# Attention B's table for permuting maxima becomes a constant of the whole kernel, loaded first, and mixer A's half outputs share one buffer

## The chip, the cores and the metric

The kernel runs on one core of a Trainium2 chip. A core has a matrix engine (TensorE, PE in the rows below, with PEld for its weight loads), a vector engine (VectorE, DVE), a scalar engine (ScalarE, ACT), a general engine (GpSimd, POOL), a sequencer that mostly issues transfers (SyncE, SP), and 16 DMA engines that the queues of all of them share. The on-chip memory is laid out in 128 partitions; matrix products end in eight banks of PSUM. The metric is the device time of one execution in microseconds (us); less is better.

## The reference, cut to what matters

One layer of a decoder over 2048 tokens of width 1024, in float32. The width is split into two groups of eight heads of 64. Mixer A is causal sliding-window attention; mixer B is dilated attention of three branches, whose maxima and denominators must be exchanged between the branches' token orders. Then output projection, a SwiGLU feed-forward part (FFN, 2816 wide) and a last normalisation.

```python
def hybrid(x):
    z = rmsnorm(x, g_attn) @ w_in + b_in          # q, k, v of A and B
    a = sliding_window_sink_gqa(qA, kA, vA, sinks)
    b = dilated_mixture(qB, kB, vB, rel_table)     # branches (128,1), (512,4), (2048,16)
    h = x + concat(rmsnorm(a, g_out_a), rmsnorm(b, g_out_b)) @ w_o
    u = rmsnorm(h, g_ffn)
    return rmsnorm(h + (silu(u @ w_gate) * (u @ w_up)) @ w_down, g_final)
```

## The kernel before

The program is written for a tile framework. A scheduler of the framework, which keeps a model of times of its own, sets the order of the instructions on each engine once, when the kernel is built; within an engine they then run strictly in that order, each waiting for semaphores. A change of pools or of one load can therefore give other orders far away from the changed lines.

The stages, by the time in the profiled execution: the input projection (up to about 310 us, with parts of mixer A's preparation), mixer A with the rest of the projections (to about 570), attention B (to about 880), the output projection (to about 1100), the first half of the FFN in two groups of tokens, `t2=0` (about 1105 to 1555) and `t2=1` (to about 1975), and the second half of the FFN to the end.

`shared_constants` loads small tensors into the pool `c0`, which lives through the whole kernel. `attend_b` opens pools of its own; its pool `cb` holds `sel`, 128 x 156 float32 (78 KB, 624 B in each partition), whose four parts are the 0/1 matrices with which `joint_max` and the sums after it permute and spread maxima among partitions. In `joint_max`, DVE builds `ex` from the maxima `nm` and `sel` (L658, L670), PE multiplies it by a part of `sel` into `pp` (L661, L672), and DVE takes the maxima (L680 to L683). ACT's exponentials of attention B (L454) wait for them. The logits of both mixers are made by L432 (PE) and L436 (DVE, which adds the bias and takes the row maxima).

SBUF is full at that place: `cb` lies where one of mixer A's work buffers (`hl` of L479) lay, so the load of `sel` can only be issued when mixer A's last units are through. It stands in SP's queue behind the loads of the first heads' `v` (L631) and ahead of the next `q` (L610).

Mixer A goes through 32 units. At the end of each, ACT copies one half of the output bank to `rawa` (L562), DVE adds the other half to it into `sums` (L565), and POOL's queue stores `sums` (L566). `rawa` has the tag `half` of the pool `qa`, which has two buffers for each tag.

In the first half of the FFN (`quads`, L1073 to L1099) both products, by the gate weights (g) and the up weights (u), are made by a Strassen-like scheme of seven products for each block of columns j, eleven blocks for each group of tokens. For each j and each of g and u there are three PSUM banks X, Y and Z; a product is 12 matmuls of 128 x 512 (four slices, three terms of split precision). Y is read twice on the way, so PE may not go on with it before DVE has read it:

```python
            product(Y, S, w, "S2", True, False)
            nc.vector.tensor_add(u2, Y, c1)          # L1082
            product(Z, S, w, "S1", True, False)
            product(Y, S, w, "S3", False, False)     # waits for u2
            nc.vector.tensor_add(u3, Y, c1)          # L1086
            nc.vector.tensor_add(c22, Z, u3)         # L1088
            product(X, S, w, "A12", False, True)
            product(Y, S, w, "A22", False, True)     # waits for u3
            nc.vector.tensor_add(c21, Y, c1)         # L1094
            product(Z, S, w, "S4", False, True)
            nc.vector.tensor_add(c12, Z, u2)         # L1098
```

DVE and ACT also prepare the weights of the next j: two raw halves of 512 KB for each of g and u are loaded by SP (`wraw_g`, `wraw_u`, L1044) into a ring of buffers that they share with the halves of `draw` (fold_down, L1135 to L1141, a third weight folded once and stored as `wT`); DVE forms `T1` to `T4` (L1050, L1052, L1056, L1060); ACT rounds (`wh`, L1035) and DVE takes the rest (`wl`, L1037). POOL, with `t2=0`, multiplies the results (L1164 to L1177) and SP stores them (`actS`, L1157). `first_quads` does the first product of `t2=0` in another way, slice by slice (L1108).

Of the kernel before, what the change touches and what calls it, by code (L numbers as in the profile page):

```python
# [10 lines left out]
F32 = mybir.dt.float32  # L11
# [6 lines left out]
P = 128  # L18
S = 2048
D = 1024  # L20
HD = 64
# [102 lines left out]

def shared_constants(tc, cp, g_out_a, g_out_b):
    nc = tc.nc
    ident = cp.tile([P, P], F32, name="ident")
    make_identity(nc, ident)  # L130
    half = cp.tile([P, 8], F32, name="half")
    nc.vector.memset(half, -0.5)
    ones = cp.tile([P, 1], F32, name="ones1")
    nc.vector.memset(ones, 1.0)
    gout = cp.tile([P, KC], F32, name="gout")
    nc.gpsimd.dma_start(gout[:, 0:4], g_out_a[0].rearrange("(k p) -> p k", p=P))
    nc.gpsimd.dma_start(gout[:, 4:8], g_out_b[0].rearrange("(k p) -> p k", p=P))
    return ident, half, ones, gout


def mixers(tc, consts, x, g_attn, w_in, b_in, sinks, rel, rope, mask_a, onehot, sel, sc):
    ident, half = consts[:2]
    with ExitStack() as e1:
        project(tc, e1, ident, half, x, g_attn, w_in, b_in, sinks, rel, rope, mask_a, onehot, sc)
    attend_b(tc, ident, sel, sc)


def project(tc, es, ident, half, x, g_attn, w_in, b_in, sinks, rel, rope, mask_a, onehot, sc):
# [269 lines left out]
def logits(nc, pools, blocks, nm, init):  # L418

    wk, _, ps_s, _, _ = pools  # L420
    nb = len(blocks)
    small = all(b["own"] for b in blocks)
    per = nb if small else 2
    nk = P if small else 2 * P
    for b0 in range(0, nb, per):
        bl = blocks[b0:b0 + per]
        s = ps_s.tile([P, per, nk], F32, tag="s", name="s")
        t = wk.tile([P, per, nk], F32, tag="t", name="t")
        for i, b in enumerate(bl):
            n = P if b["own"] else 2 * P  # L430
            for m in range(2):
                nc.tensor.matmul(s[:, i, :n], b["q"], b["k"][m], start=(m == 0), stop=(m == 1))  # L432
        for i, b in enumerate(bl):
            n = P if b["own"] else 2 * P
            c = b["col"]
            nc.vector.tensor_tensor_reduce(  # L436
                out=b["kv"](t[:, i, :n]), in0=b["kv"](s[:, i, :n]), in1=b["tab"], scale=-0.125, scalar=init,
                op0=ALU.add, op1=ALU.min, accum_out=nm[:, c:c + 1])
            b["t"] = t[:, i, :n]
# [20 lines left out]
def transposed(nc, ident, pools, blocks, ps):  # L460

    _, hp, _, ps_t, _ = pools
    nb = len(blocks)
    hl = hp.tile([P, 2, 2 * nb, P], F32R, tag="hl", name="hl")
    small = all(b["own"] for b in blocks)
    per = nb if small else 2
    for b0, p in zip(range(0, nb, per), ps):
        pt = ps_t.tile([P, 4, P], F32, tag="pt", name="pt2")
        slots = []
        for i, b in enumerate(blocks[b0:b0 + per]):  # L470
            for hfn in range(1 if b["own"] else 2):
                sl = i if small else 2 * i + (1 if b["own"] else hfn)
                nc.tensor.transpose(pt[:, sl, :], p[:, i, hfn * P:(hfn + 1) * P], ident)  # L473
                slots.append(sl)
        a, z = slots[0], slots[-1] + 1
        off = b0 if small else 2 * b0
        hi, lo = hl[:, 0, off + a:off + z, :], hl[:, 1, off + a:off + z, :]
        nc.scalar.copy(hi, pt[:, a:z, :])  # L478
        nc.vector.tensor_sub(lo, pt[:, a:z, :], hi.bitcast(F32))  # L479
    return hl  # L480
# [19 lines left out]
class MixerA:  # L500
# [22 lines left out]
    def unit(self, jg, g, h):  # L523
        nc, sc = self.nc, self.sc
        j0 = max(4 * jg - 1, 0)
        nj = 4 * jg + 4 - j0
        if h == 4 * g:
            self.k = []
            for s2 in range(2):
                k = self.kp.tile([P, 5 * P], F32R, tag=f"k{s2}", name=f"ka{s2}")  # L530
                for d in range(2):
                    nc.sync.dma_start(k[d * 64:d * 64 + 64, :nj * P].bitcast(F32),
                                      sc.kA[g, s2, :, j0 * P:(j0 + nj) * P])
                self.k.append(k)
            self.v = self.kp.tile([P, 5, P], F32R, tag="v", name="va")
            nc.sync.dma_start(self.v[:, :nj].bitcast(F32),
                              sc.vA[j0 * P:(j0 + nj) * P, g].rearrange("(j p) e -> p j e", p=P))
        if h % 2 == 0:
            self.q = self.qp.tile([P, 2, 512], F32R, tag="q", name="qa")
            nc.sync.dma_start(self.q.bitcast(F32),  # L540
                              sc.qA[h:h + 2].rearrange("h s d n -> (s d) h n")[:, :, jg * 512:(jg + 1) * 512])
        qs = self.q[:, h % 2]
        raw = self.qp.tile([HD, 512], F32, tag="half", name="rawa")
        blocks = []
        for i in range(4):
            j = 4 * jg + i
            own = j == 0
            a = j - (0 if own else 1) - j0
            blocks.append(dict(
                q=qs[:, i * P:(i + 1) * P], own=own, col=j,  # L550
                k=[k.rearrange("p (j r a) -> p r j a", r=16, a=8)[:, :, a:j + 1 - j0, :] for k in self.k],
                tab=self.mska[:, :, 8:16] if own else self.mska, kv=k1v,
                tv=ident_f if own else t1v, pv=ident_f if own else p1v))
        nm, l = self.nm[:, h], self.l[:, h]
        logits(nc, self.pools, blocks, nm, self.nsnk[:, h:h + 1])
        o = self.ps_o.tile([P, 512], F32, tag="o", name="oa")
        hl = transposed(nc, self.ident, self.pools, blocks, exps(nc, self.pools, blocks, nm, l, 2))
        weighted(nc, blocks, hl, self.v, [4 * jg + i - j0 for i in range(4)], 0 if jg else None,
                 lambda oc, w, m: (o[:, oc * P:(oc + w) * P], m), True, True)


        nc.scalar.copy(raw, o[HD:])  # L562
        r4 = raw.rearrange("p (j t n) -> p t j n", j=4, t=4)
        sums = self.qp.tile([HD, 512], F32, tag="sums", name="sums")
        nc.vector.tensor_tensor(out=sums.rearrange("p (t j n) -> p t j n", t=4, j=4), in0=o[:HD].rearrange("p (j t n) -> p t j n", j=4, t=4), in1=r4, op=ALU.add)  # L565
        nc.gpsimd.dma_start(sc.oA[:, h * HD:(h + 1) * HD, jg * P:(jg + 1) * P].rearrange("t p n -> p t n"),  # L566
                            sums.rearrange("p (t n) -> p t n", t=4))
# [12 lines left out]
        nc.gpsimd.dma_start(self.sc.fA.rearrange("t h (j n) -> (h j) t n", j=16), ft)  # L580


def attend_b(tc, ident, sel_in, sc):

    nc = tc.nc
    with ExitStack() as es:
# [5 lines left out]
        rp = es.enter_context(tc.tile_pool(name="rp", bufs=2, reuse_waits="tile"))  # L592
        st = es.enter_context(tc.tile_pool(name="st", bufs=2, reuse_waits="tile"))
        cp = es.enter_context(tc.tile_pool(name="cb", bufs=1, reuse_waits="tile"))
        sel = cp.tile([P, 28 + P], F32, name="sel")
        nc.sync.dma_start(sel, sel_in)
        mod8, div8, div32, mod32 = sel[:, 0:8], sel[:, 8:24], sel[:, 24:28], sel[:, 28:]
        rcs = cp.tile([P, NH // 2, NT, 2, 4], F32, name="rcs")
        ps_s = es.enter_context(tc.tile_pool(name="ps_s", bufs=2, space=PSUM, reuse_waits="tile"))
# [196 lines left out]
def phase3(tc, consts, x, w_o, g_ffn, w_gate, w_up, w_down, g_final, out, sc):  # L796
    nc = tc.nc
    with ExitStack() as es:
        ps = es.enter_context(tc.tile_pool(name="ps3", bufs=8, space=PSUM, reuse_waits="tile"))
        with tc.tile_pool(name="rw3", bufs=4, reuse_waits="tile") as rw:  # L800
            project_out(tc, consts, ps, rw, x, w_o, g_ffn, sc)
            ffn_in(tc, ps, rw, w_gate, w_up, w_down, sc)
        ffn_out(tc, consts, ps, w_down, g_final, out, sc)
# [9 lines left out]
def project_out(tc, consts, ps, rw, x, w_o, g_ffn, sc):  # L813

    nc = tc.nc
    ident, half, ones, gout = consts
    xr = x[0].rearrange("(i r) d -> r i d", r=16)
    wov = w_o[0].rearrange("(k p) n -> p k n", p=P)
    with ExitStack() as es:
        pool = lambda name, bufs: es.enter_context(tc.tile_pool(name=name, bufs=bufs, reuse_waits="tile"))  # L820
        op, wp0, slot, wp1, cp, sp, xp, hp = (pool(n, b) for n, b in (
            ("op", 2), ("wo30", 1), ("slot", 6), ("wo31", 1), ("c3", 1), ("s3", 2), ("x3", 8), ("hst", 2)))
# [484 lines left out]
def hybrid_layer(tc, x, g_attn, w_in, b_in, sinks, rel_table, g_out_a, g_out_b, w_o, g_ffn, w_gate, w_up, w_down,  # L1307
                 g_final, rope, mask_a, onehot, sel, out):
    with tc.tile_pool(name="scr", bufs=1, space=DRAM) as pool, tc.tile_pool(name="c0", bufs=1) as cp:
        sc = make_scratch(pool)  # L1310
        consts = shared_constants(tc, cp, g_out_a, g_out_b)
        mixers(tc, consts, x, g_attn, w_in, b_in, sinks, rel_table, rope, mask_a, onehot, sel, sc)
        phase3(tc, consts, x, w_o, g_ffn, w_gate, w_up, w_down, g_final, out, sc)


# [20 lines left out]
```

## Time and profile before

| | |
|---|---|
| time, median of 3 runs | 2415.98 us (2415.11 to 2416.64) |
| the profiled execution: its own time | 2418.04 us |
| its span in the trace | 2416.3 us |
| mean granted clock of TensorE | 0.976 of full speed |
| PE busy | 2310.1 us, 96% of the span |
| DVE, ACT, POOL busy | 1619.8, 1062.1, 498.5 us |

The span is from the first to the last instruction of the profiled execution; the other 1.7 us lie around it. "Idle before" of an instruction is the time in which its engine did nothing ahead of it, with what ended that. The granted clock is 1.00 at 2.4 GHz and 0.50 at 1.2 GHz. Durations of neighbouring instructions overlap a little: a DVE instruction of 128 x 512 is shown with 0.68 us and the next begins 0.60 us after its start.

### The profile page before, as it was taken

How to read it: one execution, taken by the hardware profiler on the slowest of the kernel's cores; microseconds unless marked ns; L12 is line 12 of the kernel's file. 1: busy time of each engine (PE TensorE's matmuls, PEld its weight loads, DVE VectorE, ACT ScalarE, POOL GpSimd, SP SyncE). 2: the span in 40 equal slices, each digit the busy share in tenths (PEclk: the TensorE clock that was granted, in tenths of full speed). 3: DMA queues.
4: the chain of work that ended last, by engine and by line, in shares of the span. 5: the costliest groups of instructions: out<-in, count | busy, mean ns of one | idle time of the engine just before them, and what ended most of it. 6: DMA issues, size and time to landing. Idle time of an engine off the chain costs nothing.

```text
span 2416.3 us, 34033 instructions
## 1 busy us (share of the span) xinstructions
PE 2310.1 (96%) x11765; PEld 1961.3 (81%) x11765; DVE 1619.8 (67%) x3155; ACT 1062.1 (44%) x2371; POOL 498.5 (21%) x446
## 2 busy tenths in 40 slices
PE   7999999997999979997999999899999999999998
PEld 7987788886999968885778878678888878888887
DVE  5335555545999986658777777696676747557555
ACT  5323355552978883434322323342323334444442
POOL 2311200001333220103223232323232330000000
PEclk9999999996999989999999999999999999999999
DMA  7657565559788667734544444343233339668663
GB/s 218 209 180 220 156 182 150 147 138 227 174 194 202 139 202 218 251 143 174 175 161 149 161 148 156 124 139 103 93 114 101 105 113 366 207 194 287 203 195 125
DMA packets 279324, 419.43 MB, mean 174 GB/s; under 512 B 24096, under 2 KB 152736, under 8 KB 274544
## 3 DMA queue, kind: packets, MB, share of 16 engines
q1 hardware_dynamic: 273216, 394.05, 53.9%
q10 hardware_dynamic: 3744, 17.11, 1.8%
q0 software_dynamic: 2192, 6.10, 1.0%
q8 instruction: 93, 1.52, 0.3%
q14 instruction: 79, 0.65, 0.1%
HBM read 278.11 MB, written 139.07 MB: 173 GB/s over the span
## 4 chain that ended last, share of the span: by engine, by line
PE 67%; DVE 15%; DMA 9%; ACT 4%; issue 3%; SPq 2%; POOL 1%; DVEq 0%; ACTq 0%; POOLq 0%
PE bY L1264 7%; PE acco L897 7%; PE acc L177 7%; PE Yg L1070 6%; PE Yu L1070 5%; PE bZ L1264 5%; PE bX L1264 5%; PE accv L244 4%; PE Zu L1070 3%; PE Xu L1070 3%; PE Zg L1070 3%; PE Xg L1070 3%; PE s L432 3%; DVE t L436 2%; ACT p L454 2%
## 5 line engine op out<-in xcount | busy, mean ns | idle before, releaser
L1217 DVE TENSOR_TENSOR o<-r,o 128x1024 fp32r<-128x1024 f32 x154 | 191.7, 1252 | 138.9 <-ACT o L1216 135.3
L1216 ACT CAST o<-r 128x1024 fp32r<-128x1024 f32 x154 | 161.1, 1049 | 228.1 <-PE bY L1264 84.3
L1164 POOL TENSOR_TENSOR c<-c,c 128x512 f32<-128x512 f32 x66 | 105.1, 1592 | 573.8 <-DVE c L1088 362.4
L1035 ACT CAST wh<-T 128x512 fp32r<-128x512 f32 x176 | 108.4, 621 | 244.9 <-PE Yg L1070 58.7
L454 ACT ACTIVATE p<-t,m 128x256 f32<-128x256 f32 (+1 forms) x384 | 176.8, 477 | 36.3 <-DVE m L682 36.1
L1264 PE MATMUL bY<-o 128*128 128x512 f32 x792 | 180.5, 389 | 0.0
L1264 PEld LDWEIGHTS bY<-o 128*128 128x128 f32 x792 | 148.7, 188 | 30.8
L177 PE MATMUL acc<-hh,wh 128*128 128x512 f32 x416 | 170.1, 409 | 0.7 <-DVE vt L247 0.7
L177 PE MATMUL acc<-hl,wh 128*128 128x512 f32 x416 | 170.1, 409 | 0.0
L177 PE MATMUL acc<-hh,wl 128*128 128x512 f32 x416 | 170.1, 409 | 0.0
L897 PE MATMUL acco<-woh,oT 128*128 128x512 f32 x512 | 164.0, 395 | 0.0
L479 DVE TENSOR_TENSOR hl<-pt,hl 128x512 fp32r<-128x512 f32 (+1 forms) x224 | 144.8, 655 | 21.9 <-ACT hl L478 21.3
L1037 DVE TENSOR_TENSOR wl<-T,wh 128x512 fp32r<-128x512 f32 x176 | 156.1, 892 | 0.6 <-ACT wh L1035 0.3
L497 PE MATMUL o<-hl,v 128*128 128x128 f32 (+1 forms) x816 | 140.8, 297 | 10.3 <-DVE hl L479 7.1
L432 PE MATMUL s<-k,q 128*128 128x256 f32 (+1 forms) x768 | 131.1, 311 | 14.8 <-DMA k<-kB 7.7
L478 ACT CAST hl<-pt 128x512 fp32r<-128x512 f32 (+1 forms) x224 | 125.1, 566 | 40.6 <-PE pt L473 39.8
L473 PE MATMUL pt<-ident,p 128*128 128x128 f32 x848 | 135.1, 285 | 4.3 <-DVE hl L479 2.7
L432 PEld LDWEIGHTS s<-k,q 128*128 128x128 f32 x768 | 112.0, 214 | 21.0 <-DVE hl L479 5.9
L1035 ACT CAST wh<-wraw_u 128x512 fp32r<-128x512 f32 x66 | 41.1, 622 | 191.1 <-PE Yu L1070 89.1
L497 PEld LDWEIGHTS o<-hl,v 128*128 128x128 f32 x816 | 113.6, 198 | 13.9 <-DVE hl L479 9.5
L1264 PE MATMUL bX<-o 128*128 128x512 f32 x528 | 120.6, 389 | 1.1 <-DVE o L1217 1.1
L1264 PE MATMUL bZ<-o 128*128 128x512 f32 x528 | 120.3, 389 | 0.0
(469 smaller groups left out, 5903.0 us busy)
## 6 DMA issues: line engine op xcount, KB each, us to landing
r<-actS SPq DMA_DIRECT2D x154, 256.0 KB
actS<-c SPq DMA_DIRECT2D x128, 256.0 KB
wraw_g<-in_w_gate_dram SPq DMA_DIRECT2D x44, 512.0 KB
wraw_u<-in_w_up_dram SPq DMA_DIRECT2D x44, 512.0 KB
r<-wT SPq DMA_DIRECT2D x88, 256.0 KB
r<-in_w_down_dram SPq DMA_DIRECT2D x66, 256.0 KB
k<-kB SPq DMA_DIRECT2D x32, 512.0 KB
draw<-in_w_down_dram SPq DMA_DIRECT2D x22, 512.0 KB
```

The costliest lines, as they stand in the source:

```text
L177: nc.tensor.matmul(acc, a[:, k, :], mv, start=(n == 0), stop=(n == 3 * KC - 1))
L432: nc.tensor.matmul(s[:, i, :n], b["q"], b["k"][m], start=(m == 0), stop=(m == 1))
L454: nc.scalar.activation(b["pv"](p[:, i, :n]), b["tv"](b["t"]), AF.Exp, scale=-1.0, bias=nm[:, c:c + 1], accum_out=l[:, c:c + 1])
L479: nc.vector.tensor_sub(lo, pt[:, a:z, :], hi.bitcast(F32))
L497: nc.tensor.matmul(out, v[:, vi, :], mov, start=(first and n == 1), stop=(last and n == 2 * len(jobs)))
L897: nc.tensor.matmul(acc, oT[t, g][kk // 2][:, kk % 2, a, i * P:(i + 1) * P], b[:, kk, :], start=(n == 0), stop=(n == 11))
L1035: nc.scalar.copy(hi, src)
L1037: nc.vector.tensor_sub(lo, src, hi.bitcast(F32))
L1070: nc.tensor.matmul(bank, a[:, k], b[:, k], start=(first and m == 0), stop=(m == 11), skip_group_check=not first)
L1216: nc.scalar.copy(o[:, 0], r)
L1217: V.tensor_sub(o[:, 1], r, o[:, 0].bitcast(F32))
L1264: nc.tensor.matmul(bank[i], o[:, u, 0, i * P:(i + 1) * P], o[:, v, 1, :], start=(first and j == 0 and m == 0), stop=(j == NP - 1 and m == ...
```

## The change

`sel` moves from `attend_b`'s pool `cb` to `c0`, and its load from SP's queue in the middle of the kernel to POOL's queue at the start, behind the two loads of `gout`. `rawa` gets one buffer in place of two, which gives back 2048 B in each partition during mixer A. What it computes stays the same.

```diff
-def shared_constants(tc, cp, g_out_a, g_out_b):
+def shared_constants(tc, cp, g_out_a, g_out_b, sel_in):
...
     nc.gpsimd.dma_start(gout[:, 4:8], g_out_b[0].rearrange("(k p) -> p k", p=P))
-    return ident, half, ones, gout
+    sel = cp.tile([P, 28 + P], F32, name="sel")
+    nc.gpsimd.dma_start(sel, sel_in)
+    return ident, half, ones, gout, sel
...
-    attend_b(tc, ident, sel, sc)
+    attend_b(tc, ident, consts[4], sc)
...
-        raw = self.qp.tile([HD, 512], F32, tag="half", name="rawa")
+        raw = self.qp.tile([HD, 512], F32, tag="half", name="rawa", bufs=1)
...
-def attend_b(tc, ident, sel_in, sc):
+def attend_b(tc, ident, sel, sc):
...
         cp = es.enter_context(tc.tile_pool(name="cb", bufs=1, reuse_waits="tile"))
-        sel = cp.tile([P, 28 + P], F32, name="sel")
-        nc.sync.dma_start(sel, sel_in)
         mod8, div8, div32, mod32 = sel[:, 0:8], sel[:, 8:24], sel[:, 24:28], sel[:, 28:]
```

Lines from L141 to L596 have numbers higher by 2 in the changed kernel. The orders of all engines are the same in both up to the names, apart from a few neighbours that change places, in all but two places. The first is the start of attention B. On DVE, the last sum of mixer A (`sums`), the first `ex` made with `sel`, and the logits of the first head (L436) stand there, before the change:

```order
664 L436 ISA nm 128x1
665 L436 ISA t,nm<-s,tab_5513 128x256
666 L436 ISA nm 128x1
667 L565 TENSOR_TENSOR sums<-oa,rawa 64x512
668 L670 TENSOR_TENSOR ex_5728<-nm,sel 128x128
669 L436 ISA t,nm<-s,tab_5513 128x128
670 L436 ISA nm 128x1
```

After it, the same `ex` stands 49 rows earlier, ahead of the logits of mixer B's last but one block, and the last `sums` keeps its place further down (L567, row 668):

```order
616 L438 ISA nm 128x1
617 L438 ISA t,nm<-s,tab_5513 128x256
618 L438 ISA nm 128x1
619 L670 TENSOR_TENSOR ex_5728<-nm,sel 128x128
620 L438 ISA t,nm<-s,tab_5513 128x128
621 L438 ISA nm 128x1
622 L438 ISA t,nm<-s,tab_5513 128x128
```

PE's product of it (L672) moves up with it, by 48 matmuls. The second place is the group `t2=0` of the FFN's first half, where the order of DVE, PE and ACT changes from the first block to the last, and SP's in some neighbours: the load of the second half of `wraw_g` now stands ahead of the store of `c22` (`actS`). On DVE, block 2, between `T2` made from the second half of `wraw_g` (L1052) and `u2` read from `Yg` (L1082), before the change:

```order
1997 L1037 TENSOR_TENSOR wl<-wraw_g,wh 128x512
1998 L1052 TENSOR_TENSOR T_13288<-wraw_g,T_13286 128x512
1999 L1094 TENSOR_TENSOR c_12943<-Yu,c_12871 128x512
2000 L1037 TENSOR_TENSOR wl<-wraw_u,wh 128x512
2001 L1098 TENSOR_TENSOR c_12964<-Zu,u_12885 128x512
2002 L1037 TENSOR_TENSOR wl<-T_13134,wh 128x512
2003 L1056 TENSOR_TENSOR T_13298<-wraw_g 128x512
2004 L1037 TENSOR_TENSOR wl<-T_13132,wh 128x512
2005 L1136 TENSOR_TENSOR draw<-draw 128x512
2006 L1060 TENSOR_TENSOR T_13308<-wraw_g,T_13288 128x512
2007 L1082 TENSOR_TENSOR u_13039<-Yg,c_13025 128x512
```

After it, the same block, from `u3` read from `Yu` (L1086) on:

```order
1995 L1086 TENSOR_TENSOR u_12911<-Yu,c_12871 128x512
1996 L1037 TENSOR_TENSOR wl<-wraw_g,wh 128x512
1997 L1088 TENSOR_TENSOR c_12913<-Zu,u_12911 128x512
1998 L1037 TENSOR_TENSOR wl<-wraw_u,wh 128x512
1999 L1052 TENSOR_TENSOR T_13288<-wraw_g,T_13286 128x512
2000 L1082 TENSOR_TENSOR u_13039<-Yg,c_13025 128x512
2001 L1037 TENSOR_TENSOR wl<-T_13134,wh 128x512
```

And block 3 of the changed kernel, from the last step of `wl` on:

```order
2034 L1037 TENSOR_TENSOR wl<-wraw_g,wh 128x512
2035 L1037 TENSOR_TENSOR wl<-wraw_u,wh 128x512
2036 L1052 TENSOR_TENSOR T_13596<-wraw_g,T_13594 128x512
2037 L1094 TENSOR_TENSOR c_13251<-Yu,c_13179 128x512
2038 L1136 TENSOR_TENSOR draw<-draw 128x512
2039 L1037 TENSOR_TENSOR wl<-T_13442,wh 128x512
2040 L1056 TENSOR_TENSOR T_13606<-wraw_g 128x512
2041 L1098 TENSOR_TENSOR c_13272<-Zu,u_13193 128x512
2042 L1082 TENSOR_TENSOR u_13347<-Yg,c_13333 128x512
```

Before, blocks 2 to 9 all have those eight rows between; after, even blocks have none (`u2` stands right behind `T2`) and odd blocks have five. One row, `wl<-wraw_u`, has moved ahead of `T2`. In block 2, `u3<-Yu` has two more rows ahead of it after the change (`gate`, L1164, and a `wl`). In block 0, two results of `first_quads` stand ahead of the `wl` that the first products wait for.

PE's order goes with it. Counted in matmuls, what lies between the end of Yu's product S3 and the start of Yg's product S3, which waits for `u2<-Yg`, is 88 in blocks 2 to 9 before the change; after it, 59 in even blocks and 73 in odd ones. Between Yu's S3 and Yu's A22, which waits for `u3<-Yu`, there are 23 in both.

## Rows read from the trace of the kernel before

**Rows 1.** The page: busy times, 40 slices of PE and its clock, chain by engine.

```profile
PE 2310.1 (96%) x11765; PEld 1961.3 (81%) x11765; DVE 1619.8 (67%) x3155; ACT 1062.1 (44%) x2371; POOL 498.5 (21%) x446
...
PE   7999999997999979997999999899999999999998
...
PEclk9999999996999989999999999999999999999999
...
PE 67%; DVE 15%; DMA 9%; ACT 4%; issue 3%; SPq 2%; POOL 1%; DVEq 0%; ACTq 0%; POOLq 0%
```

**Rows 2.** Timeline of the start of attention B, several engines.

```profile
586.85 1.82 SPq L596 DMA_DIRECT2D sel<-in_sel_dram  x1
...
587.61 0.68 DVE L565 TENSOR_TENSOR sums<-oa,rawa 64x512 f32<-64x512 f32 x1
...
588.77 0.38 SPq L610 DMA_DIRECT2D q<-qB  x1
595.05 0.29 DVE L670 TENSOR_TENSOR ex<-nm,sel 128x128 f32<-128x128 f32 x1 [6.76 <-DMA sel<-in_sel_dram]
...
595.40 0.61 PE L672 MATMUL pp<-sel,ex 128*128 128x16 f32 x2 [5.96 <-DVE ex L670]
...
597.53 2.29 POOL L653 CAST q<-q 128x512 fp32r<-128x512 f32 x4 [8.32 <-PE s L432]
```

**Rows 3.** Stretches from mixer A's end into attention B, busy us and counts.

```profile
core 0: us, PE busy (x) PEld busy (x) DVE busy (x) ACT busy (x) POOL busy (x), PEclk, DMA share, GB/s
...
570.00:588.00 18.00, 17.52 (x74) 15.85 (x74) 12.37 (x74) 0.00 (x0) 2.90 (x5) 0.50 1.07 220
...
589.40:595.00 5.60, 0.04 (x1) 0.00 (x0) 0.00 (x0) 0.00 (x0) 0.00 (x0) 0.50 0.97 243
595.00:607.00 12.00, 10.94 (x47) 10.04 (x48) 9.14 (x54) 3.17 (x13) 2.29 (x4) 0.50 0.76 173
607.00:620.00 13.00, 12.83 (x109) 12.30 (x107) 12.20 (x52) 12.97 (x50) 2.37 (x4) 0.99 0.17 38
```

**Rows 4.** Timelines of ACT and DVE at mixer A's last units.

```profile
549.10 0.68 DVE L565 TENSOR_TENSOR sums<-oa,rawa 64x512 f32<-64x512 f32 x1
...
551.54 0.58 ACT L562 COPY rawa<-oa 64x512 f32<-64x512 f32 x1 [0.23 <-PE oa L497]
...
573.52 0.68 DVE L565 TENSOR_TENSOR sums<-oa,rawa 64x512 f32<-64x512 f32 x1
...
567.80 0.58 ACT L562 COPY rawa<-oa 64x512 f32<-64x512 f32 x1 [1.33 <-PE oa L497]
603.83 0.40 ACT L454 ACTIVATE p<-t,m 128x128 f32<-128x128 f32 x1 [35.45 <-DVE m L682]
```

**Rows 5.** Timeline of the first microseconds.

```profile
1.30 0.93 POOL L136 DMA_DIRECT2D gout<-in_g_out_a_dram  x1 [0.36 <-issue]
1.86 4.78 SPq L219 DMA_DIRECT2D xt<-in_x_dram  x4
2.23 0.77 POOL L137 DMA_DIRECT2D gout<-in_g_out_b_dram  x1
3.08 0.31 POOL masks.py:199 TENSOR_SCALAR_AFFINE_SELECT ident<-ident 128x128 f32<-128x128 f32 x1
...
8.62 1.23 DVE L223 CUSTOM_DVE_ANT_0 sq<-xt 128x1024 f32<-128x1024 f32 x1 [7.72 <-DMA xt<-in_x_dram]
...
11.54 1.97 PE L233 MATMUL pt<-ident,xt 128*128 128x128 f32 x8 [11.54 <-DVE xt L228]
```

**Rows 6.** PE's waits from 1105 to 1545 us: total us, times, longest.

```profile
PE Yg L1070 <- DVE u L1082: 7.1, 5, 4.3
...
PE Yu L1070 <- DVE u L1086: 1.7, 1, 1.7
...
PE Xu L1070 <- DVE wl L1037: 1.1, 1, 1.1
...
PE Yu L1070 <- DVE wl L1037: 0.9, 1, 0.9
```

**Rows 7.** Timelines of DVE and PE in block 2.

```profile
1189.14 0.69 DVE L1052 TENSOR_TENSOR T<-wraw_u,T 128x512 f32<-128x512 f32 x1 [2.47 <-DMA wraw_u<-in_w_up_dram]
...
1192.31 0.68 DVE L1086 TENSOR_TENSOR u<-Yu,c 128x512 f32<-128x512 f32 x1
...
1194.71 1.45 DVE L1037 TENSOR_TENSOR wl<-wraw_g,wh 128x512 fp32r<-128x512 f32 x1
1201.44 0.69 DVE L1052 TENSOR_TENSOR T<-wraw_g,T 128x512 f32<-128x512 f32 x1 [5.28 <-DMA wraw_g<-in_w_gate_dram]
...
1207.69 0.39 PE L1070 MATMUL Xu<-A11h,wh 128*128 128x512 f32 x1
...
1211.68 0.68 DVE L1082 TENSOR_TENSOR u<-Yg,c 128x512 f32<-128x512 f32 x1
...
1212.42 0.79 PE L1070 MATMUL Yg<-S3h,wh 128*128 128x512 f32 x1 [4.34 <-DVE u L1082]
```

**Rows 8.** Stretches around that wait, columns as in rows 3.

```profile
1212.00:1218.00 6.00, 5.58 (x13) 4.42 (x14) 2.69 (x5) 0.06 (x1) 0.89 (x1) 0.50 0.23 87
1218.00:1225.00 7.00, 7.00 (x31) 5.72 (x31) 4.66 (x8) 3.31 (x6) 0.00 (x0) 0.98 0.50 158
```

**Rows 9.** Timelines of PE and DVE in block 7, a steady one.

```profile
1387.24 0.39 PE L1070 MATMUL Yu<-S3l,wh 128*128 128x512 f32 x1
...
1389.53 0.69 DVE L1086 TENSOR_TENSOR u<-Yu,c 128x512 f32<-128x512 f32 x1
...
1391.93 1.46 DVE L1037 TENSOR_TENSOR wl<-wraw_g,wh 128x512 fp32r<-128x512 f32 x1
1397.37 0.69 DVE L1052 TENSOR_TENSOR T<-wraw_g,T 128x512 f32<-128x512 f32 x1 [3.98 <-DMA wraw_g<-in_w_gate_dram]
...
1399.78 1.19 DVE L1037 TENSOR_TENSOR wl<-T,wh 128x512 fp32r<-128x512 f32 x1
1401.00 1.66 DVE L1056 TENSOR_TENSOR T<-wraw_g 128x512 f32<-128x512 f32 x1
1402.59 1.77 DVE L1037 TENSOR_TENSOR wl<-T,wh 128x512 fp32r<-128x512 f32 x1
...
1407.68 0.68 DVE L1082 TENSOR_TENSOR u<-Yg,c 128x512 f32<-128x512 f32 x1
```

More of the change, by code (lines that the diff above doesn't have):

```diff
@@ L137, in shared_constants, with mixers @@
     nc.gpsimd.dma_start(gout[:, 4:8], g_out_b[0].rearrange("(k p) -> p k", p=P))
-    return ident, half, ones, gout
-def mixers(tc, consts, x, g_attn, w_in, b_in, sinks, rel, rope, mask_a, onehot, sel, sc):
+    sel = cp.tile([P, 28 + P], F32, name="sel")
+    nc.gpsimd.dma_start(sel, sel_in)
+    return ident, half, ones, gout, sel
+def mixers(tc, consts, x, g_attn, w_in, b_in, sinks, rel, rope, mask_a, onehot, sc):
     ident, half = consts[:2]
@@ L815, in project_out @@
     nc = tc.nc
-    ident, half, ones, gout = consts
+    ident, half, ones, gout = consts[:4]
     xr = x[0].rearrange("(i r) d -> r i d", r=16)
@@ L1310, in hybrid_layer @@
         sc = make_scratch(pool)
-        consts = shared_constants(tc, cp, g_out_a, g_out_b)
-        mixers(tc, consts, x, g_attn, w_in, b_in, sinks, rel_table, rope, mask_a, onehot, sel, sc)
+        consts = shared_constants(tc, cp, g_out_a, g_out_b, sel)
+        mixers(tc, consts, x, g_attn, w_in, b_in, sinks, rel_table, rope, mask_a, onehot, sc)
         phase3(tc, consts, x, w_o, g_ffn, w_gate, w_up, w_down, g_final, out, sc)
```

## The prediction

> **What bounds the kernel now.** The page comes first: PE is busy 96% of the span and holds 67% of the chain that ended last; the other engines have room [rows 1]. So time is to be had only where PE stands still or runs at half its clock, and the slices show few such places. I looked for them in the stretches, at the waits of PE, and at the timeline ahead of each wait. Two bear on this change.
>
> The first is the start of attention B. DVE ends mixer A's last sum at 588.3 us (587.61 + 0.68) and then stands for 6.76 us, because the next row on it needs `sel`, whose load was issued at 586.85 and landed at about 595; PE stands for 5.96 us behind it [rows 2]. From 589.4 to 595.0 no engine works [rows 3]. The second is the FFN's first half with `t2=0`. From 1105 to 1545 us PE waits 7.1 us in five waits for `u2<-Yg`, one of 4.3 us, and 1.7, 1.1 and 0.9 us in three others [rows 6].
>
> **The change, part by part.** The sum is made against the profiled execution's own 2418.04 us, which is 2.06 us above the median of the three runs; I take the 2.06 off at the end.
>
> *The load at the start.* POOL issues one more DMA. The two of `gout` took 0.93 and 0.77 us of POOL, so the mask of `ident` behind them starts at about 3.9 in place of 3.08 us; PE first needs `ident` at 11.54, so this is hidden by 7 us [rows 5]. Not hidden is the transfer: DVE's first work waits until 8.62 us for the first `xt`, of which four were issued from 1.86 on [rows 5]. The first `xt` is 512 KB and arrived 6.8 us after the issue began; 78 KB beside it, at that rate, is at most 1.0 us, and nothing if the `xt` gets its share first. I take +0.4 (0 to +1.0).
>
> *The wait for `sel`.* It goes: the tile is there from the start, and its readers need nothing else that is late. The `ex` now stands ahead of the logits of another block, after the sum at 573.52, where its 0.29 us are at no one's cost: PE is the busy engine there (17.52 of 18 us, DVE 12.37) [rows 3, 4]. What is late next? `q`, `k` and the first exponentials all wait for PE or DVE themselves (the cast of `q` started at 597.53 behind PE's logits [rows 2]), so they move with the wait. PE is the bound in the stretch, so its 5.96 us are the lower end and DVE's 6.76 the upper. I take −6.4 (−6.8 to −6.0). SP also has one row less ahead of `q`, whose load has more slack than that row's 1.82 us.
>
> *One buffer for `rawa`.* The copy of a unit (L562) now waits for the sum of the unit before it (L565). I set the 32 copies against the 32 sums: 30 of the 31 that have one ahead started 1.76 to 17.2 us after its end, the closest being the copy at 551.54 after the sum at 549.10, and wait for nothing. Only the last copy started too early, at 567.80; the sum ahead of it ends at 574.2, so it waits 6.4 us [rows 4]. Behind it on ACT is the first exponential, which comes at 603.83 after 35.45 idle us; the sum that needs this copy stands at 587.61 [rows 2, 4]. The copy would end at 574.8, 13 us ahead of the sum and 22 ahead of the exponential (with the gain above taken off): 0. The Trainium skill (Trainium Kernel Development and Optimization, Best Practices) asks for double buffers, so that transfers overlap with work; by that rule a second buffer less costs time. No run shows it for this tile; these rows show 6.4 us of delay and no one who waits for it.
>
> *The new order of the FFN's first half.* It is a by-product, and the larger unknown. In block 2 before the change: DVE ends `wl<-wraw_g` at 1196.2, only then can the next half of `wraw_g` be loaded, `T2` starts on it 5.28 us later at 1201.44, and `u2<-Yg`, eight rows behind, at 11.68 − 1.44 = 10.24 us after that [rows 7]. PE had gone through its other products by 1207.9 and stood 4.34 us. After it the clock was at half: 13 matmuls took 5.58 us, where 31 take 7.00 at full clock, so 13 would take 2.94: another 2.6 us [rows 8]. In the new order `u2` is the row right behind `T2`. `u3<-Yu` to the end of `u2` is then: one row 0.6, `wl` to `T2` 1.45 + 5.28, `T2` 0.6, `u2` 0.7, together 8.6 us. PE starts A22 about 0.75 after `u3` starts and has 36 matmuls of 0.2265 us, 8.2, before S3: 8.9 us. It just fits, so I take −6.9 (−6.9 to 0).
>
> The same reckoning for the other blocks. The other four waits for `u2<-Yg` are 7.1 − 4.3 = 2.8 us together [rows 6]. In even blocks the path from `u3` to `u2` falls from 18.15 us (1389.53 to 1407.68) to about 0.6 + 5.44 + 0.6 = 6.6, while PE arrives (88 − 59) × 0.2265 = 6.6 us sooner: 5 us more slack, no wait. In odd blocks DVE has `gate`, a `wl`, `c22` (with the first row 2.4), 5.44 from `wl` to `T2`, and `T2`, `c21`, `draw`, `wl`, `T3`, `c12`, which are 5.3 to 6.9 us, as POOL's work stretches those with operands in SBUF alone from 0.68 to 1.2 and 1.77 [rows 9]: 13.1 to 14.7 in place of 18.15, and 0.7 for `u2`. PE has 73 × 0.2265 = 16.5 us from the end of Yu's S3. `u3` was 2.1 us late behind it in block 7 (1389.53 against 1387.24 + 0.2). So odd blocks have between +2.7 and −1.0 us. Four odd blocks: the term is −2.8 to +1.2; I take −2.0.
>
> Block 0: two rows of 0.6 us come ahead of the `wl` for which PE waits 1.1 and 0.9 us already [rows 6]; both on the path: +1.2 (0 to +2.4). Block 2 has two more rows ahead of `u3<-Yu`, for which PE waited 1.7 us: +1.2 if nothing else moves, −1.7 if the load of `wraw_u`, for which DVE waited 2.47 us before it [rows 7], comes sooner; I take +0.6.
>
> Sum: +0.4 − 6.4 + 0 − 6.9 − 2.0 + 1.2 + 0.6 = −13.1 us. 2418.04 − 13.1 − 2.06 = 2402.9 us. The bounds together are −18.2 and +1.0 − 6.0 + 2.4 + 1.2 + 1.2 = −0.2, that is 2397.8 to 2415.8.
>
> **The rivals.**
> *The FFN gains nothing.* The scheduler's new order removes one wait and makes others: block 2's margin is 0.3 us, and with the long load it fails by a little; odd blocks wait 1 us. Then only `sel` and the start count: −6.0, and with waits as before 2410; with the +1.8 of blocks 0 and 2 as well 2411.8. For it: the margins above are below the error of such a reckoning. Against: the rows between `T2` and `u2` are gone.
>
> *More is gained.* PE's clock is at half from before mixer A's end until 607 [rows 3]. If it rises when work goes on without the gap, up to half of the 10.94 us of the 47 matmuls of 595 to 607 is saved, 5.5 us: 2397.4. The Trainium skill (TensorE: Matmul & The Clock Gate, What's actually happening) says that throttled is the default and that sustained work releases it, which by itself is for this rival. Against it stand the rows: in 570 to 588 PE was busy 17.52 of 18 us and the clock stayed at 0.50 [rows 3].
>
> *Slower.* In odd blocks `c12<-Zu` stands ahead of `u2<-Yg` on DVE; if `T2`'s load comes late there (the loads share SP's queue with the stores), PE waits 4.3 us and loses 2.6 at half clock, as block 2 did. Four of them are 27.6 us, less the 2.8 of the waits of before, in place of −2.0: 2402.9 + 26.8 = 2429.7. Slower than before by 4.8 us is reached when each of the four loses 4.7 us. Against it: 73 matmuls leave 16.5 us, and the estimate is at most 17.5.
>
> *The wait only changes its name.* Something else of attention B's start (the first heads' loads, with a DMA share near 1.0 until 595 [rows 3]) is late by the same amount: −13.1 + 6.4 gives 2409.3. Against it: what waits there waits for PE and DVE.
>
> **How the numbers follow.** A measurement of this kernel tells 0.2%, 4.8 us, from no change. Forecast 0.55 (2398 to 2408, faster). FFN gains nothing 0.18 (2409 to 2415: half faster, half same). More gained 0.10 (2393 to 2398, faster). Wait renamed 0.10 (2406 to 2413; seven in ten faster). Slower 0.07. That is faster 0.55 + 0.09 + 0.10 + 0.07 = 0.81, of which I give 0.03 to same for the errors of the sum: 0.78; same 0.09 + 0.03 + 0.03 = 0.15; slower 0.07. The range 2396 to 2416 leaves out the slower case and part of the one that gains more.
>
> **What would show it.** Right: no idle time ahead of the `ex` with `sel`; attention B's stages 6 to 7 us sooner; PE's waits for `u2<-Yg` below 1 us each; full clock at about block 2; the last `rawa` copy late, with no one waiting. Wrong: a wait for `q`, `k` or `v` near 590 us; PE's waits for `u2` or `u3` in the FFN above 7.1 us in sum; the first `xt` later than 8.62 by over 1 us.

## The result, and the profile after

The changed kernel takes 2397.92 us in the median of four runs (2390.97 to 2400.54), the kernel before, run beside it, 2415.55. The ratio is 0.9925 with a 95% interval of [0.9901, 0.9949]: 18 us faster, where 13 were forecast. The profiled execution took 2399.05 us with a span of 2397.3.

The page of the changed kernel, the lines of [rows 1]:

```profile
PE 2302.2 (96%) x11765; PEld 1954.8 (82%) x11765; DVE 1608.9 (67%) x3155; ACT 1062.1 (44%) x2371; POOL 494.1 (21%) x447
...
PEclk9999999997999979998999999999999999999999
...
PE 74%; DVE 11%; DMA 6%; ACT 4%; issue 3%; SPq 1%; POOL 1%; DVEq 0%; POOLq 0%; ACTq 0%
```

DVE and DMA have lost shares of the chain that ended last to PE (the chain is followed back from the last instruction, at each step to what released it): less of its time goes to them. The span is 19 us shorter.

The start of attention B in the changed kernel's timeline, against [rows 2, 4]:

```profile
576.99 0.68 DVE L567 TENSOR_TENSOR sums<-oa,rawa 64x512 f32<-64x512 f32 x1
...
577.77 0.58 ACT L564 COPY rawa<-oa 64x512 f32<-64x512 f32 x1 [7.71 <-DVE sums L567]
...
579.07 0.29 DVE L670 TENSOR_TENSOR ex<-nm,sel 128x128 f32<-128x128 f32 x1
...
587.91 0.68 DVE L567 TENSOR_TENSOR sums<-oa,rawa 64x512 f32<-64x512 f32 x1
...
591.09 2.29 POOL L653 CAST q<-q 128x512 fp32r<-128x512 f32 x4 [1.58 <-PE s L434]
...
597.39 0.40 ACT L456 ACTIVATE p<-t,m 128x128 f32<-128x128 f32 x1 [19.04 <-DVE m L682]
```

The `ex` with `sel` has no idle time ahead of it. The last copy to `rawa` now waits for the sum of the unit before, which ends at 577.67; ACT had stood for 7.71 us and then stands for another 19.04, and the sum that reads the copy comes ten microseconds later, at 587.91. The first exponential comes at 597.39 in place of 603.83, though mixer A's end came 3.6 us later in this execution than in the one of [rows 2].

PE's waits from 1105 to 1545 us in the changed kernel, against [rows 6]:

```profile
PE Xu L1070 <- DVE wl L1037: 1.7, 1, 1.7
PE Yu L1070 <- DVE u L1082: 0.9, 1, 0.9
...
PE Xu L1070 <- ACT c L1079: 0.3, 1, 0.3
```

The 7.1 us of waits for `u2<-Yg` are gone, the 1.7 us for `u3<-Yu` too; one of 0.9 us for `u2<-Yu` has come. Block 2 on DVE, against [rows 7]:

```profile
1187.34 0.69 DVE L1086 TENSOR_TENSOR u<-Yu,c 128x512 f32<-128x512 f32 x1
1187.94 0.68 DVE L1037 TENSOR_TENSOR wl<-wraw_g,wh 128x512 fp32r<-128x512 f32 x1
...
1192.46 0.69 DVE L1052 TENSOR_TENSOR T<-wraw_g,T 128x512 f32<-128x512 f32 x1 [2.63 <-DMA wraw_g<-in_w_gate_dram]
1193.07 0.69 DVE L1082 TENSOR_TENSOR u<-Yg,c 128x512 f32<-128x512 f32 x1
```

From the start of `u3` to the end of `u2` it is 6.4 us, where before it was 20.1 (1192.31 to 1212.36). The prediction had 8.6: `wl` took 0.68 us and not 1.45, as no POOL work ran beside it in this order, and the load's share of the wait was shorter.

### The profile page after: what moved, and what is told of

Its sections match the earlier page's. It is cut to its first block, busy times and chain, and to the rows that moved or that the text cites. A ratio compares the mean times of both kernels' runs of the same rounds, so it can differ in the third digit from the quotient of the medians.

```text
span 2397.3 us, 34036 instructions
## 1 busy us (share of the span) xinstructions
PE 2302.2 (96%) x11765; PEld 1954.8 (82%) x11765; DVE 1608.9 (67%) x3155; ACT 1062.1 (44%) x2371; POOL 494.1 (21%) x447
## 4 chain that ended last, share of the span: by engine, by line
PE 74%; DVE 11%; DMA 6%; ACT 4%; issue 3%; SPq 1%; POOL 1%; DVEq 0%; POOLq 0%; ACTq 0%
PE bY L1264 7%; PE acco L897 7%; PE Yu L1070 7%; PE acc L179 7%; PE Yg L1070 6%; PE bZ L1264 5%; PE bX L1264 5%; PE Zu L1070 5%; PE Xu L1070 4%; PE Zg L1070 4%; PE Xg L1070 4%; PE accv L246 4%; PE s L434 3%; DVE t L438 2%; PE pt L475 2%
## 5 line engine op out<-in xcount | busy, mean ns | idle before, releaser
L1164 POOL TENSOR_TENSOR c<-c,c 128x512 f32<-128x512 f32 x66 | 103.9, 1575 | 571.3 <-DVE c L1088 391.2
L434 PE MATMUL s<-k,q 128*128 128x256 f32 (+1 forms) x768 | 125.0, 299 | 16.6 <-DVE hl L481 6.2
L499 PEld LDWEIGHTS o<-hl,v 128*128 128x128 f32 x816 | 114.7, 200 | 14.4 <-DVE hl L481 9.8
L434 PEld LDWEIGHTS s<-k,q 128*128 128x128 f32 x768 | 106.0, 202 | 22.9 <-DVE hl L481 6.3
L438 DVE CUSTOM_DVE_ANT_0 t<-s,tab 128x256 f32<-128x256 f32 (+1 forms) x344 | 112.6, 370 | 7.4 <-PE s L434 4.8
```

The lines of the kernel that those rows point to most:

```text
L438: nc.vector.tensor_tensor_reduce(out=b["kv"](t[:, i, :n]), in0=b["kv"](s[:, i, :n]), in1=b["tab"], scale=-0.125, scalar=init, op0=ALU.add, ...
L499: nc.tensor.matmul(out, v[:, vi, :], mov, start=(first and n == 1), stop=(last and n == 2 * len(jobs)))
```

## The experiments

Two edits and a by-product (the FFN's order) act at once. Small edits to the first loads change the scheduler's order or leave it, which lets sel's arrival and the order be set apart: e1, e5 and e6 have the late `sel` and the old order, e2 the early `sel` and mostly the old order of the FFN, e3 the late `sel` and the new order, the changed kernel both. In e2, e7, e8 and e10 the order at the end of attention B differs as well, which is taken up under e9 and e10.

**e1: one buffer for `rawa` alone.**

```diff
-        raw = self.qp.tile([HD, 512], F32, tag="half", name="rawa")
+        raw = self.qp.tile([HD, 512], F32, tag="half", name="rawa", bufs=1)
```

> Mixer A's half outputs in one buffer, sel loaded as before; the order of all engines is that of before, row for row. My theory (the wait of the last copy is hidden): within 0.2% of before, 2411 to 2420 us; ACT's last rawa copy starts at about 574 in place of 567.8, and DVE's wait for sel of 6 to 7 us is still there. Rival (the one buffer costs or gains something by itself): outside 0.2%, with more than 1 us of waits for rawa in mixer A.

Measured: 2417.39 us against 2417.44, ratio 1.0005 [0.9995, 1.0015]. In its timeline the last copy waits, and so does DVE for `sel`:

```profile
571.57 0.58 ACT L562 COPY rawa<-oa 64x512 f32<-64x512 f32 x1 [7.84 <-DVE sums L565]
...
590.51 0.29 DVE L670 TENSOR_TENSOR ex<-nm,sel 128x128 f32<-128x128 f32 x1 [8.49 <-DMA sel<-in_sel_dram]
```

The one buffer costs and gains nothing that this interval (−0.05 to +0.15%) would show. The copy starts at 571.57, not at about 574, as all of mixer A's end came 2.7 us sooner in this trace. The wait for `sel` was 8.49 us, longer than the 6 to 7 expected; e5 bears on that.

**e2: `sel` early, the FFN's order nearly as before.** The changed kernel with the load on ACT's queue:

```diff
-    nc.gpsimd.dma_start(sel, sel_in)
+    nc.scalar.dma_start(sel, sel_in)
```

> sel kept with the constants and loaded first, but by ACT's queue in place of POOL's; the scheduler then gives the FFN's first half nearly the order of before (block 2 has five rows in place of eight between T2 and u2, blocks 3 to 9 have the eight of before). Theory (sel and FFN are two gains of their own): only attention B's start gains, 6 to 11 us: 2405 to 2410; PE's waits for u2 from Yg in the FFN stay at 2 us or more. Rival (the whole gain hangs on sel): as the changed kernel, 2398.

Measured: 2404.40 us, ratio 0.9947 [0.9933, 0.9960]. This is 0.6 us below the range of the theory and 6 us above the rival's 2398. PE's waits in the FFN stay. Its waits from 1105 to 1545 us and its timeline in block 3, the first block there with eight rows between `T2` and `u2`, show them:

```profile
PE Yg L1070 <- DVE u L1082: 5.5, 6, 3.1
...
1238.17 0.50 PE L1070 MATMUL Yg<-S3h,wh 128*128 128x512 f32 x1 [3.10 <-DVE u L1082]
```

Block 2, with five rows, has no such wait in this kernel: the long wait went to the first block that has the eight rows.

**e3: `sel` late, the new order.** The kernel before with one buffer for `rawa` and a load that nobody reads:

```diff
-def shared_constants(tc, cp, g_out_a, g_out_b):
+def shared_constants(tc, cp, g_out_a, g_out_b, sel_in):
...
+    pad = cp.tile([P, 28 + P], F32, name="pad")
+    nc.gpsimd.dma_start(pad, sel_in)
     return ident, half, ones, gout
...
-        raw = self.qp.tile([HD, 512], F32, tag="half", name="rawa")
+        raw = self.qp.tile([HD, 512], F32, tag="half", name="rawa", bufs=1)
...
```

> sel stays with attention B and its late load on SP's queue, rawa has one buffer, and POOL's queue loads a second copy of sel at the start that nobody reads. The orders are those of the changed kernel but for two rows (the ex and its product are where they were before). Theory: attention B's start waits for sel as before, the FFN gains about 10 us: 2404 to 2408; no wait for u2 from Yg over 0.5 us. Rival (the new order only gains when the program comes 7 us earlier to the FFN): within 0.2% of before.

Measured: 2405.04 us, ratio 0.9944 [0.9929, 0.9960]. The wait for `sel` is there, the waits for `u2<-Yg` are not:

```profile
586.69 1.89 SPq L598 DMA_DIRECT2D sel<-in_sel_dram  x1
...
594.31 0.29 DVE L672 TENSOR_TENSOR ex<-nm,sel 128x128 f32<-128x128 f32 x1 [9.68 <-DMA sel<-in_sel_dram]
...
PE Yu L1072 <- DVE u L1084: 1.7, 1, 1.7
PE Xu L1072 <- DVE wl L1039: 1.7, 1, 1.7
```

So the new order gains by itself, also when the program does not come to the FFN some 7 us sooner.

**e4: the changed kernel again.**

> The changed kernel once more. Theory (two gains that add up): the sum of the gains of e2 and e3, 2396 to 2400 us; the trace has the same stages within 1 us, apart from stretches of half clock. Rival (part of the 18 us is chance in one profiled execution): 2403 or more in the median.

Measured: 2400.21 us, ratio 0.9929 [0.9914, 0.9944], 17 us under the kernel before and 0.2 above the theory's range. By their medians the two gains do not add up: 13.0 (e2) and 12.4 (e3) are 25 together. The stages of e2's trace say why its gain is larger than that of `sel` alone: against the trace of before it is 6.2 us shorter at attention B's start, but also 2.4 in the FFN (a part of its order is new) and 4.5 between attention B's first product and the FFN. The last is a gain that the changed kernel does not have (see e9 and e10). The second trace of the changed kernel is not within 1 us of the first in the FFN: it is 1.5 us longer there, with 4.4 us more at half clock.

**e5, e6: more traces of the old order.** e5 is the kernel before; e6 is e1 with an unused tile:

```diff
+    cp.tile([P, 28 + P], F32, name="pad")
     return ident, half, ones, gout
...
```

> The kernel before once more, for a second trace. If the stretch of full clock within mixer A's tail (10 to 14 us long, between 570 and 586 us, seen in the changed kernel and where rawa alone has one buffer) is chance, this trace may show it too, and DVE's wait for sel is then longer (8 to 10 us) while attention B starts no sooner. If it hangs on one of the edits, this trace is at half clock from 556 to 607 us as the first one, with a wait of 6 to 7 us.

> rawa in one buffer and an unused tile of sel's size among the constants; sel as before; the orders are those of before, row for row. Theory (the FFN's order came from one more load ahead in the scheduler's reckoning, not from addresses): PE's waits for u2 from Yg in the FFN are 7 to 8 us as before, the time within 0.2% of before. For the clock of mixer A's tail it is one more trace: full in part if one buffer for rawa is what does it, half if it is chance.

Measured in one run each: 2413.38 and 2410.06 us, a little below the 2414.51 to 2418.30 of the kernel before in those rounds. For e6 this is 0.3%, more than the 0.2% expected, which a single run cannot settle. The waits for `u2<-Yg` are 7.2 us (longest 2.9) in e5 and 5.8 (longest 2.0, less than expected) in e6, and e6 has the order of before on DVE, ACT and PE: other addresses alone do not make the FFN's new order, nor end its waits. In e5 the clock of mixer A's tail is at full from 576 on, unlike [rows 3], and the kernel is the same:

```profile
570.00:575.00 5.00, 4.78 (x21) 4.23 (x20) 4.17 (x20) 0.00 (x0) 0.18 (x1) 0.50 1.01 228
576.00:588.00 12.00, 8.18 (x57) 6.86 (x56) 7.48 (x51) 0.00 (x0) 2.35 (x5) 1.00 1.10 231
588.00:600.00 12.00, 5.81 (x24) 5.22 (x24) 5.51 (x34) 0.00 (x0) 2.29 (x4) 0.57 0.84 214
```

DVE's wait for `sel` is then 8.12 us. PE is through sooner and stands longer: the load's landing, not PE, sets the time there. The expectation that attention B starts no sooner than in the first trace does not hold: its start takes 40.91 us in place of 44.15 (table below).

**e7, e8: other first loads.** e7 has the load on SP's queue; e8 keeps the tile with the constants and writes the load in `attend_b`:

```diff
# e7
-    nc.gpsimd.dma_start(sel, sel_in)
+    nc.sync.dma_start(sel, sel_in)
# e8, against the changed kernel
-    nc.gpsimd.dma_start(sel, sel_in)
...
# in attend_b
+        nc.sync.dma_start(sel, sel_in)
         mod8, div8, div32, mod32 = sel[:, 0:8], sel[:, 8:24], sel[:, 24:28], sel[:, 28:]
```

> sel with the constants and loaded first, by SP's queue ahead of gcol and x in place of POOL's. Theory: attention B's gain as in the changed kernel, the FFN's order like that of the changed kernel but for some 38 rows on DVE, so 2397 to 2404 us; x comes at most 1 us later. Rival (SP's queue is dear at the start): the first xt comes over 1 us later and the time is above 2404.

> sel's buffer with the constants, its load written at the start of attend_b on SP's queue as before; with its buffer free from the start, the scheduler puts it at SP's row 10, among the first loads of x. Theory (the buffer alone, not the place in the code, made sel late): no wait for sel; attention B gains 6 to 11 us; the FFN has a third order, in which block 2 has T2 and u2 next to each other as in the changed kernel: 2396 to 2404 us. Rival (the FFN's gain is particular to the order of the changed kernel): PE waits over 3 us for u2 there, 2405 or more.

Measured: 2394.17 us, ratio 0.9907 [0.9890, 0.9923], and 2400.35 us, ratio 0.9932 [0.9917, 0.9947]. e7 is 3 us faster than its theory, and its first `xt` comes at 9.76 us, 1.1 later than before and so just outside what was expected. Both have no wait for `sel` and none over 0.2 us for `u2<-Yg`. e8 says that the buffer made `sel` late, and not the place in the code: with a free buffer the scheduler takes the load to the start (8.75 us in e8).

What the buffer set, by the scheduler's reckoning, was the load's place in SP's queue; when the kernel before ran, the rows show the queue ahead of the load, and not the buffer:

```profile
565.81 1.95 PE L497 MATMUL oa<-hl,va 128*128 128x256 f32 x8
...
568.31 18.43 SPq L631 DMA_DIRECT2D v<-vR  x4
```

Mixer A's last product with `hl` ends at 567.8, 19 us ahead of the load. In between SP issues four loads of `v`, the first alone for 14.4 us, and the load of `sel` follows right behind them, at 586.85 [rows 2]. A kernel with the late load ahead of those of `v` was not run.

**e9, e10: the changed kernel and e7 on one chip.**

> The changed kernel a third time, beside e10 on the same chip. Theory: 2396 to 2402 us, as the two times before.

> sel loaded first by SP's queue once more, to tell it from the changed kernel. If POOL's queue costs the changed kernel something (e7 had 2394.2 where the changed kernel had 2397.9 and 2400.2 in other rounds), it is 3 to 6 us faster than e9 with intervals that do not meet; if that was chance between rounds, the two agree within 0.15% (3.6 us). By the orders nothing speaks for a difference over 1 us.

Measured: 2398.69 us, ratio 0.9915 [0.9891, 0.9939], and 2393.82 us, ratio 0.9906 [0.9885, 0.9927]. e9 is as expected. The medians are 4.9 us apart (e7 was 3.8 and 6.0 us under the changed kernel in other rounds), but the intervals overlap for the most part, and one run of e9 took 2388.87. Neither of the two cases expected of e10 holds: `sel` on SP's queue beats the kernel before, and by the times alone it stays open whether it beats the changed kernel.

The traces show where a difference lies. From the first product `o` of attention B to the FFN, e7 and e10 take 491.2 and 491.3 us (e2 491.1), and the eight traces with the orders of before, e3 and the changed kernel 493.4 to 498.5. Against the changed kernel it arises between 840 and 900 us, at the end of attention B, where the order of the products `o` and of ACT's work ahead of them is another one (the one such place on PE and ACT behind attention B's start). One sort of PE's waits from 790 to 905 us, in the changed kernel and in e7:

```profile
PE o L499 <- ACT hl L480: 3.2, 2, 1.6
...
PE o L499 <- ACT hl L480: 0.6, 1, 0.6
```

All of PE's waits there are 17.7, 18.9 and 19.3 us in the three traces of the changed kernel, 14.6 and 14.8 in e7 and e10. So the orders do differ where the time does, by more than the 1 us expected. That the order is the cause is not shown, as no run changes it alone.

e9 also has a trace with the early `sel` in which the clock of mixer A's tail stays at half, though PE is as busy at 570 to 575 as in e5:

```profile
570.00:575.00 5.00, 4.83 (x22) 4.30 (x21) 4.29 (x20) 0.58 (x1) 1.87 (x4) 0.50 1.01 280
576.00:588.00 12.00, 11.64 (x52) 10.94 (x52) 8.03 (x53) 0.00 (x0) 0.33 (x2) 0.50 1.11 213
588.00:600.00 12.00, 11.50 (x53) 10.41 (x53) 9.16 (x54) 3.78 (x16) 2.61 (x5) 0.52 0.97 260
```

With these, two stages can be set against each other over the traces: the start of attention B, from PE's transposition of `pfa` (L577) to the first product `o` of head 0 (L497), and the FFN's first half, from the first matmul of `t2=0` (FA) to the tenth of the twelve of `t2=1`'s first product A22 into Yg. Each entry is the difference of two start times in the trace, in us.

```
trace                  clock in tail   attention B's start   FFN
before                 half            44.15                 521.4
e5 (before)            partly full     40.91                 521.9
e1 (late, old)         partly full     41.20                 522.3
e6 (late, old)         partly full     41.25                 519.3
e3 (late, new)         partly full     43.64                 509.9
e2 (early, mixed)      half            37.92                 519.0
after (early, new)     partly full     33.68                 510.2
e4 (after)             partly full     33.68                 511.7
e9 (after)             half            37.82                 510.9
e7 (early, new)        partly full     33.82                 512.4
e10 (early, new)       partly full     33.77                 512.2
```

(In e8, where the clock is full in part, the two are 38.12 and 511.4; its order has 184 matmuls in attention B's start, the others 164.)

## Why the prediction was right, point by point

The profiled executions before and after, in the stages of the table, with what the prediction took for each (us):

```
stage                                before   changed   difference   taken
start to `pfa`                       565.75   569.35    +3.6         +0.4
attention B's start                   44.15    33.68   −10.5         −6.4
from there to FA                     495.66   495.02    −0.6         none
the FFN's first half                 521.38   510.23   −11.2         −7.1
the rest                             789.32   789.00    −0.3         none
span                                2416.26  2397.28   −19.0        −13.1
```

**The wait for `sel`: right, and its size depends on the clock.** Taken: −6.4 us. With the tail at half clock, before against e2 and e9 is 44.15 to 37.92 and 37.82: −6.2 and −6.3. With a part at full clock, the late `sel` has 40.91 to 43.64 and the early one 33.7 to 33.8: −7 to −10. Over all eleven traces the means are 42.2 late and 35.1 early: −7.1, near the term. With the FFN's −10.0 (below) this is −17.1, and the medians of the three rounds gave −17.6, −17.2 and −18.0. So the −10.5 of the profiled pair has chance in it: the execution before was one of three traces at half clock, and the one after was not. The rival that more is gained was half right: the stretch of full clock is worth about 4.2 us with the early `sel` (37.9 to 33.7) and 0.5 to 3.2 with the late one, as the wait for `sel` (6.76, 8.12 to 9.68 us) takes up what PE saves. But the stretch does not come from the missing gap: e5 has it with the gap and e9 has it not without one. The Trainium skill (TensorE: Matmul & The Clock Gate, What's actually happening) says that sustained work releases the clock. That does not tell these traces apart: from 570 to 575 us PE was busy 4.78 of 5 us in e5, which rose, and 4.72 in the first trace of the same kernel and 4.83 in e9, which did not.

**One buffer for `rawa`: right.** The copy waits, nobody waits for it (e1: 1.0005 [0.9995, 1.0015]).

**The load at the start: not to be told from chance.** Taken: +0.4 us. `ident`'s mask starts at 3.63, the first `xt` arrives at 8.81 in place of 8.62. Between 0 and 566 us, traces of one order differ by more than the term: the changed kernel's three came 3.6 and 2.1 us later and 1.4 us sooner than the one before.

**The FFN: the right mechanism, too small.** The sum of its terms was −6.9 − 2.0 + 1.2 + 0.6 = −7.1 us. The seven traces with a new order have 511.2 us in the mean, the four with the old one 521.2: −10.0. PE does the same number of matmuls in every order, so the traces can be compared at the n-th matmul after FA's first; a difference there says how far PE is behind (+) or ahead (−), in us:

```
n                                      108      432     1836     2109
lies in the trace of before, us       1143     1225     1548     1627
changed − before, profiled pair       +1.5     −6.6    −10.7    −11.2
mean of seven new − mean of four old  +1.4     −4.7     −9.1    −10.0
```

- The first products of block 0 (to n = 108) were to cost 1.2 and cost 1.5 in the pair, 1.4 in the means.
- The stretch from there through block 2 (to 432) was to gain 6.9 − 0.6 = 6.3. It gains 8.1 in the pair and 6.1 in the means. The long wait was not the same in every execution of the old order: 4.34 us in [rows 7], 4.4 in e1, but 2.9 in e5 and 2.0 in e6. In the changed kernel it is gone, and the clock does not fall between 1132 and 1538 us. `u3<-Yu` was to cost 0.6; in place of its wait of 1.7 us there is one of 0.9 for `u2<-Yu`. The last three steps of the folding of `draw` stand together in the new order, `wraw_u` is loaded sooner, and DVE waits 0.70 us for it in place of 2.47.
- The steady blocks (to 1836) were to gain 2.0 of the 2.8 us of waits. They gain 4.1 in the pair and 4.4 in the means. This is the term that was mis-sized: in the changed kernel no odd block waits, which is 0.8, and a stop of PE costs more than the idle time that the trace gives it, which is 1.0. PE at the wait of block 7, before the change:

```profile
1407.19 0.39 PE L1070 MATMUL Xu<-A11h,wh 128*128 128x512 f32 x1
1408.41 0.50 PE L1070 MATMUL Yg<-S3h,wh 128*128 128x512 f32 x1 [0.83 <-DVE u L1082]
1408.74 0.39 PE L1070 MATMUL Yg<-S3h,wl 128*128 128x512 f32 x1
```

In a run of matmuls each starts 0.2265 us after the one before. Here one starts 1.22 us after it and the next 0.33: 1.1 us are lost where 0.83 are shown as idle. By the starts of the matmuls the four waits of 2.8 us cost 3.8.

- The rest, −0.5 and −0.9, comes where `t2=0` gives way to `t2=1`, for which the prediction had no term.

The forecast's range held 2397.92 by 1.9 us only, and the band with most of the chance, 2398 to 2408, begins just above it. Its lower bound had no room for the stretch of full clock, which was set aside as a rival by the one trace that happened not to have it, nor for an FFN gain of 10 us. One reading in the working is off without weight: by its row the last matmul ahead of the long wait ends at 1208.1, not 1207.9.

Not settled: what lets the clock rise in mixer A's tail in some executions, and whether the other order at the end of attention B is what puts the medians of e7 and e10 below the changed kernel's.

## What to carry to other kernels

Look for the DMA that ends an idle time of all engines, and ask what set its place in its queue. Here it was a buffer that lay where earlier work had its own: with a buffer of its own the load went to the start although it was written in the same place (e8). Where a scheduler sets the order, one more load at the start can change the order a millisecond later (e3 does, an unused tile of the same size does not), so read the new order on each engine and cost it as a change of its own. Before a stage is sized from one trace, see whether its clock is the same in a second one. And size a stop of PE by the starts of its matmuls, not by the idle time shown.

## What the runs showed of the hardware

Two executions of the same program can differ by a stretch of 10 to 14 us at full clock in the same place, with PE equally busy before it (4.72 and 4.78 of 5 us in the two of the kernel before); in eight of the eleven traces of the table it was there. Between 556.0 and 607.2 us the clock of the first of these stayed at half, though PE was busy 17.52 of the 18 us from 570 to 588 [rows 3].

While an instruction of POOL runs, DVE's 128 x 512 instructions with all operands in SBUF take up to 1.77 us in place of 0.68 [rows 9]; those that read PSUM are not hit (`u2<-Yg` at 1407.68 takes 0.68 us beside POOL's 1407.16 to 1408.88). Which of them are hit is a matter of the order, and in block 2 it was worth 0.8 us on the path to the next load.

A stop of PE at full clock costs about 0.27 us more than its idle time in the trace, by the four waits of the steady blocks: a 128 x 512 matmul is shown with 0.39 us but in a run the next starts 0.2265 us after it, and the first one after the stop holds up the second to 0.33 us.
